# Gate and up projections of a decoder block: tokens as the stationary operand, weights as the moving one

## The chip, the cores and the metric

One core of a Trainium2 chip runs the whole block in one launch. The metric is the device time of one execution in microseconds (us). The three timed runs of the kernel before lie between 1873.48 and 1873.96 us, with the median at 1873.7 us.

## The reference

One decoder layer on 512 tokens with a model width of 2048, in float32. The first half (RMSNorm, three token mixers, output projection, residual) is not touched by the change. The second half is:

```python
h2 = _rms_norm(x, norm2_g[l])
x = x + (jax.nn.silu(h2 @ w_gate[l]) * (h2 @ w_up[l])) @ w_down[l]
```

`w_gate` and `w_up` are 2048 x 5632 (44 blocks of 128 hidden channels each), and `w_down` is 5632 x 2048.

## The kernel before, in words

The float32 products are made of three products of rounded parts (`F32R`): high x high, high x low, low x high. An operand tile `h` or `a` (128 x 512) therefore holds 256 columns of high parts and then 256 of low parts. Weights come from DRAM as plain float32 tiles of 128 x 1024 ("raw": `w('21', 'g10')` and so on). ScalarE rounds each of them twice (`wn` into PSUM, L293, and `wh` into SBUF, L294), and VectorE makes the low part `wl` (L295). The kernel calls one such tile in its split form a unit.

The three big products are done by a Strassen-Winograd scheme. Tokens are cut into two halves of 256, and the other two dimensions into two halves as well. Instead of eight block products there are seven, in the fixed order `ORDER = (5, 1, 7, 6, 2, 4, 3)`. The sums of weight blocks that the scheme needs (`s = 21+22`, `21 += 11`, `s += 11`, `s += 12`) are made by GpSimd (L200 for gate and up, L241 for down). The sums of the operands are made once, during the output projection that precedes (`operand`, L1100 to L1110), for all eight pairs of input blocks: 56 tiles `h`, of which `h7_3` is product 7, pair 3. They stay in SBUF through gate and up.

Gate and up (class `Wide`, L1308). There are 44 groups: pairs `p` of hidden blocks in `GU_ORDER`, gate first (`g10`) and then up (`u10`). A group has seven products, each with one unit. A product is 8 matmuls of 512 columns (`wh` stands in the array, the high and low columns of `h` move) and 8 of 256 columns (`wl` stands, the high columns move), all at L1292. Results lie with hidden channels on partitions. VectorE adds them out of PSUM (L1300 to L1334), GpSimd multiplies by the tokens' norm (`R_21`, L1258 and L1345), ScalarE applies SiLU, GpSimd multiplies gate and up. The pieces `sums1` to `piece4` then make the seven operand tiles `a` of the down projection. For all pairs but 0 and 5 (`STAY`) these tiles go out to DRAM (`od`) and are read back later.

Down. For the first 16 of 22 pairs (class `Turned`, 8 steps) it is done the other way round: blocks of 128 tokens of `a` stand, and 512 columns of weights move (L1434: 4 hidden or output blocks of 128 columns each). A step has 7 products with two units each, and a unit is 12 matmuls of 512 columns. Two banks are written per product, and the next product writes the other two. Its `a` tiles are read back from `od` every second step. The last 6 pairs (class `Down`) have the form of `Wide` again.

Order of the work: everything is written in program order per engine. `split_up_to` keeps the split `SPLIT_AHEAD = 2` units ahead of TensorE. `pump` issues weight loads on SP's queue as soon as a raw buffer of the right kind is free in the program's order. `later(n, ...)` puts work n products later, into `evacs` (emptying PSUM) or `extras` (the rest). All loads and stores stand in SP's one queue in program order, and SP waits in order. `SUMS_AT` says how many units ahead of a group each weight sum is made.

Of the kernel before, what the change touches and what calls it, by code (L numbers as in the profile page):

```python
# [53 lines left out]

SUMS_AT = {1: [(-4, -3, 0, 2)], 2: [(-5, -2, 1, 5), (-3, -1, 2, 6)]}
# [20 lines left out]
GU_ORDER = [*range(1, 5), *range(6, NP), 0, 5]  # L76
STAY = (0, 5)
# [6 lines left out]
RINGS = {"22": ("22a", "x0", "22b"), "s": ("sa", "x1", "sb"), "21": ("21", "x2"), "1": ("11", "x3", "12")}  # L84
# [38 lines left out]
def kernel(ctx: ExitStack, tc: tile.TileContext, xT, wi, wo, wgu, wd, cst_in, outT):  # L123
# [41 lines left out]
    first_sum, opening = [], f"g{GU_ORDER[0]}"  # L165
# [19 lines left out]

    def group(name, m, n, blocks):

        key = {k: (k, name) for k in ("11", "12", "21", "22", "s")}
        for k in ("21", "22", "11", "12"):
            entries.append((k + "ab"[m] if k == "22" else k, key[k], blocks[k]))  # L190
        u = len(works)

        def add(to, a, b, last=None):
            def go():
                if to == a:
                    out = raws[key[to]][0]
                else:
                    out = take("s" + "ab"[m], key[to], n)
                eng = nc.vector if name == opening and b == "11" and to == a == "s" else nc.gpsimd
                eng.tensor_add(out[:, :n], raws[key[a]][0][:, :n], raws[key[b]][0][:, :n])  # L200
                if last:
                    drop(key[last])
            return go

        sums[u - 4].append(add("s", "21", "22"))
        sums[u - 3].append(add("21", "21", "11"))
        if name == opening:
            first_sum.append((add("s", "s", "11"), key["11"]))
        else:
            sums[u].append(add("s", "s", "11", "11"))  # L210
        sums[u + 2 + (name == opening)].append(add("s", "s", "12"))
        works.extend((key[k], last, None) for k, last in (
            ("s", False), ("11", False), ("21", True), ("s", False), ("12", True), ("22", True), ("s", True)))

    for p in GU_ORDER:
        for m in range(2):
            group(f"{'gu'[m]}{p}", m, 1024, {f"{i + 1}{k + 1}": [wgu[4 * (p + i * NP) + 2 * m + k]]
                                             for i in range(2) for k in range(2)})
# [7 lines left out]
    def down_group(name, n, subs):  # L226
# [19 lines left out]
        for i in range(many):  # L246
            at_sum = SUMS_AT[many][i] if name != "d0" or i else (-4, *SUMS_AT[many][i][1:])
# [847 lines left out]
    x2d = {n: tc.dram_tile([P, T], F32, name=f"x2d{n}") for n in range(KT)}  # L1095

# [3 lines left out]
    def operand(q, j, src):  # L1100
        if q == 5 and j < N_WIDE:
            if j % 2 == 0:
                opening_ops[j] = wide(j + 1, f"h5_{j}", F32R)
            t = ops[q, j] = opening_ops[j - j % 2][:, j % 2 * T:(j % 2 + 1) * T]
        else:
            t = ops[q, j] = slot(f"h{q}_{j}", F32R)
        hi, lo = halves(t)
        nc.scalar.copy(hi, src)
        nc.vector.tensor_sub(lo, src, hi.bitcast(F32))

# [85 lines left out]
    for half in range(2):  # L1196
        for i, n in enumerate(OUT_ORDER[half]):
# [11 lines left out]
            if half == 1 and i == KT - 1:  # L1209
                drop(first_sum[0][1])  # L1210
            for kk in range(8):
                if half == 1 and i == KT - 2 and kk == 4:
                    first_sum[0][0]()
# [21 lines left out]
    r2b = cp.tile([P, 3 * TH], F32, name="r2b")  # L1235
    R_12, R_21, R_1, R_2 = r2b[:, :T], r2b[:, TH:], r2b[:, :TH], r2b[:, TH:T]
# [4 lines left out]
    def norm2a():  # L1241
        n2["b"] = psum["high"].tile([P, 1024], F32, name="n2s", tag="h")
        n2["r"] = token_scale(ssum2, D, "n2", n2["b"][:, :NT])[1]

    def norm2b():
        b = spread(n2["r"], "r2s", n2.pop("b")[:, T:])
        nc.scalar.copy(R_12, b)
        nc.scalar.copy(r2b[:, T:], b[:, :TH])
# [59 lines left out]
    class Wide(Block):  # L1308


        def __init__(self, p, m, gate):
            super().__init__(f"{'gu'[m]}{p}", m)
            self.p, self.gate = p, gate

        def done(self, q):
            if q == 1:
                self.u = slot(f"{self.name}u")
                self.u1, self.u2 = halves(self.u)
                self.both(1, self.u1)
            elif q == 7:  # L1320
                self.l, self.r = slot(f"{self.name}l"), slot(f"{self.name}r")
                self.both(7, self.r[:, :TH])
                self.add(5, self.r[:, :TH], sign=nc.vector.tensor_sub)
            elif q == 6:
                self.add(6, self.u2, self.u1)
                nc.gpsimd.tensor_sub(self.r[:, :TH], self.r[:, :TH], self.u2)
            elif q == 2:
                self.both(2, self.r[:, TH:])
                self.finish(self.r, self.gate and self.gate.r)
            elif q == 4:  # L1330
                c21 = self.l[:, TH:]
                main, rest = halves(self.banks[4])
                nc.vector.tensor_sub(c21, main, self.u2)
                nc.vector.tensor_add(c21, c21, rest)  # L1334
            elif q == 3:
                self.add(3, self.l[:, :TH], self.u2)
                self.u = self.u1 = self.u2 = None
                self.finish(self.l, self.gate and self.gate.l)
                if self.gate:
                    for n, piece in ((0, self.sums1), (1, self.piece3), (3, self.piece1), (4, self.sums2),  # L1340
                                     (6, self.piece2), (8, self.piece4)):
                        later(n, piece, queue=extras)

        def finish(self, t, gate):
            nc.gpsimd.tensor_mul(t, t, gate if gate is not None else R_21)  # L1345
            if gate is None:
                later(0, nc.scalar.activation, t, t, AF.Silu, queue=extras)
                later(1, nc.gpsimd.tensor_mul, t, t, R_21, queue=extras)


        def sums1(self):
            self.gate = None
# [11 lines left out]
        def piece(self, at, src):  # L1364
# [6 lines left out]
            for k in range(n):  # L1371
# [5 lines left out]
                if self.p in STAY:  # L1377
                    acts[q, self.p] = t
                else:
                    later(0, nc.sync.dma_start, od[self.p][:, (at + k) * T:(at + k + 1) * T], t.bitcast(F32),  # L1380
                          queue=extras)
# [121 lines left out]

    class Down(Block):
# [48 lines left out]
    def load_act(q, pairs):  # L1553
        for j in pairs:
            if j in STAY:
                continue
# [4 lines left out]
    blk = gate = None  # L1561
    rest = [(q, j) for q in ORDER for j in range(TURNED, NP)]
    for buf in ("x1", "x3"):
        held[buf] = "ops"
    for g in range(2 * NP + N_DOWN):
        t = g - 2 * NP
        turned = 0 <= t < N_TURNED
        if t < 0:
            p, m = GU_ORDER[g // 2], g % 2
            blk = Wide(p, m, gate if m else None)  # L1570
            gate = blk if m == 0 else None
        else:
            blk = (Turned if turned else Down)(t)
        for i, q in enumerate(ORDER):
            sums_now()
            run(evacs)
            for sub in range(BY // 2 if turned else 1):
                w = next_unit(SPLIT_AHEAD - (g == 0 and i == 2))
                if g == 0 and ticks.due:
                    for first in (0, NJ // 2):  # L1580
                        blk.multiply(q, w, [ops[q, j] for j in range(first, first + NJ // 2)], first, first > 0)
                        ticks.tick()
                elif t < 0:
                    blk.multiply(q, w, [ops[q, j] for j in range(NJ)])
# [5 lines left out]
            if g == 0 and i in (2, 3):  # L1590
                (norm2a, norm2b)[i - 2]()

            if t == -2 and i in (3, 6):
                load_act(ORDER[i // 6], range(BY))
            if t == -1:
                for j in range(NJ):
                    ops.pop((q, j))
                if i == 1:
                    held.pop("x1"), held.pop("x3")
                    opening_ops.clear()  # L1600
                if i < len(ORDER) - 2:
                    later(1 if i < len(ORDER) - 3 else 3, load_act, ORDER[i + 2], range(BY), queue=extras)
# [100 lines left out]
```

## Time and profile before

| | |
|---|---|
| median of 3 runs | 1873.7 us (1873.48 to 1873.96) |
| the profiled execution: its own time | 1876.25 us |
| the profiled execution: span of the core | 1874.5 us |
| TensorE busy in the span | 1867.3 us |
| VectorE, ScalarE, GpSimd busy | 1454.2, 1329.0, 1217.9 us |
| granted TensorE clock | 1.00 in every slice |
| moved by DMA | 301.07 MB, 161 GB/s on average |

The profile is one execution on the chip. Busy time is the union of an engine's instructions. Matmuls overlap: one of 512 columns is listed with 389 ns, and the next one starts 227 ns later, so a price of a matmul is read from starts or from counts per stretch and not from its duration. "PEld" is the loading of the standing operand, which overlaps with matmuls.

### The profile page before, as it was taken

The page shows a single profiled execution, that of the slowest core. Times are in us where ns is not written, and L with a number is a line of the kernel's source. Part 1 is how long each engine was busy: PE and PEld are TensorE (multiplying, and loading weights), DVE is VectorE, ACT ScalarE, POOL GpSimd, SP SyncE. Part 2 cuts the span into 40 slices and gives each one's busy share as a digit, 9 for nine tenths or more (in the row PEclk, how much of TensorE's full clock was granted, in tenths as well). Part 3 has the DMA queues.
Part 4 walks back from the last instruction along what each step waited for, and adds up shares of the span by engine and source line. Part 5 has one row for each costly group of instructions (what it writes and reads, how often), then busy time and mean ns, then how long its engine had stood idle before and what let it go on. Part 6 is the DMA issues. An engine that isn't in the chain of part 4 may idle for free.

```text
span 1874.5 us, 28274 instructions
## 1 busy us (share of the span) xinstructions
PE 1867.3 (100%) x9784; PEld 1604.5 (86%) x9784; DVE 1454.2 (78%) x2267; ACT 1329.0 (71%) x1870; POOL 1217.9 (65%) x796
## 2 busy tenths in 40 slices
PE   9999999999999999999999999999999999999999
PEld 7888888888888888888888888888888888888888
DVE  7688899897589777777777777777777677778887
ACT  6325556454466888888888888888888887777675
POOL 5003444362155887887878878778787767766786
PEclk9999999999999999999999999999999999999999
DMA  7334333433342353544535445354455465578984
GB/s 260 124 107 114 101 97 107 113 119 119 104 155 91 123 181 130 167 159 145 176 130 169 157 148 174 129 172 155 150 171 201 150 233 189 194 257 283 309 241 124
DMA packets 157984, 301.07 MB, mean 161 GB/s; under 512 B 29968, under 2 KB 69008, under 8 KB 157840
## 3 DMA queue, kind: packets, MB, share of 16 engines
q1 hardware_dynamic: 157696, 299.25, 48.8%
q8 instruction: 77, 1.26, 0.3%
q14 instruction: 67, 0.55, 0.1%
q10 hardware_dynamic: 144, 0.01, 0.0%
HBM read 241.27 MB, written 50.33 MB: 156 GB/s over the span
## 4 chain that ended last, share of the span: by engine, by line
PE 95%; DVE 3%; issue 1%; ACT 0%; DMA 0%; SPq 0%; DVEq 0%; ACTq 0%
PE out L1292 51%; PE out L1434 16%; PE o L332 2%; PE o L331 2%; PE o L333 2%; PE cq L331 2%; PE cq L332 2%; PE cq L333 2%; PE in L331 1%; PE in L332 1%; PE in L333 1%; PE aq L331 1%; PE bu L332 1%; PE aq L333 1%; PE bu L331 1%; PE bu L333 1%
## 5 line engine op out<-in xcount | busy, mean ns | idle before, releaser
L1292 PE MATMUL out<-h,wh 128*128 128x512 f32 x2464 | 588.4, 391 | 0.0
L1292 PEld LDWEIGHTS out<-h,wh 128*128 128x128 f32 x2464 | 452.7, 188 | 87.5
L1292 PEld LDWEIGHTS out<-h,wl 128*128 128x128 f32 x2464 | 316.2, 191 | 12.5 <-DVE wl L295 0.4
L1292 PE MATMUL out<-h,wl 128*128 128x256 f32 x2464 | 320.3, 283 | 0.2 <-DVE wl L295 0.2
L1434 PE MATMUL out<-wh,a 128*128 128x512 f32 x896 | 221.3, 389 | 0.0
L1434 PEld LDWEIGHTS out<-wh,a 128*128 128x128 f32 x896 | 168.2, 188 | 34.9
L1434 PE MATMUL out<-wl,a 128*128 128x512 f32 x448 | 119.7, 389 | 0.0
L1434 PEld LDWEIGHTS out<-wl,a 128*128 128x128 f32 x448 | 84.1, 188 | 17.4
L533 DVE SCALAR_TENSOR_TENSOR y<-bu,cst,y 128x511 f32<-128x511 f32 (+14 forms) x120 | 93.8, 782 | 1.4
L289 ACT CAST wh<-w 128x1024 fp32r<-128x1024 f32 (+1 forms) x41 | 42.1, 1032 | 59.0 <-PE o L332 34.5
L1292 PE MATMUL out<-a,wh 128*128 128x512 f32 x330 | 80.1, 391 | 0.0
L309 ACT CAST wh<-w 128x1024 fp32r<-128x1024 f32 x52 | 54.8, 1053 | 32.1 <-PE bg L332 9.0
L313 DVE TENSOR_TENSOR wl<-w,wh 128x1024 fp32r<-128x1024 f32 x52 | 65.3, 1257 | 14.2 <-ACT wh L309 13.9
L1292 PEld LDWEIGHTS out<-a,wh 128*128 128x128 f32 x330 | 60.2, 188 | 11.4
L290 DVE TENSOR_TENSOR wl<-w,wh 128x1024 fp32r<-128x1024 f32 (+1 forms) x41 | 51.6, 1260 | 11.9 <-ACT wh L289 11.7
L331 PE MATMUL o<-mh_c,wh 128*128 128x512 f32 x128 | 51.2, 400 | 0.0
L332 PE MATMUL o<-ml_c,wh 128*128 128x512 f32 x128 | 50.2, 392 | 0.1
L333 PE MATMUL o<-mh_c,wl 128*128 128x512 f32 x128 | 50.1, 392 | 0.0
L1479 DVE TENSOR_TENSOR Y<-Y,out 128x512 f32<-128x512 f32 x48 | 30.8, 683 | 19.4 <-PE out L1434 19.3
L1292 PEld LDWEIGHTS out<-a,wl 128*128 128x128 f32 x330 | 43.3, 191 | 2.2
L1292 PE MATMUL out<-a,wl 128*128 128x256 f32 x330 | 44.0, 283 | 0.0
L449 POOL TENSOR_TENSOR ssum<-ssum,sq 128x512 f32<-128x512 f32 x15 | 25.9, 1725 | 22.1 <-ACT sq L448 21.6
(3358 smaller groups left out, 5235.7 us busy)
## 6 DMA issues: line engine op xcount, KB each, us to landing
od<-a SPq DMA_DIRECT2D x140, 256.0 KB, 4.8
a<-od SPq DMA_DIRECT2D x140, 256.0 KB, 6.2
w<-in_wi SPq DMA_DIRECT2D x59, 512.0 KB, 3.5
w<-in_wo SPq DMA_DIRECT2D x32, 512.0 KB, 3.5
x<-in_xT SPq DMA_DIRECT2D x16, 256.0 KB, 7.1
xr<-in_xT SPq DMA_DIRECT2D x16, 256.0 KB, 3.9
x2d<-xr SPq DMA_DIRECT2D x16, 256.0 KB, 2.0
yd<-z SPq DMA_DIRECT2D x16, 256.0 KB, 5.3
```

The lines of the kernel that those rows point to most:

```text
L289: nc.scalar.copy(hi[:, :n], t[:, :n])
L290: eng.tensor_sub(lo[:, :n], t[:, :n], hi[:, :n].bitcast(F32))
L309: nc.scalar.copy(hi, t)
L313: nc.vector.tensor_sub(lo, t, hi.bitcast(F32))
L331: nc.tensor.matmul(out, wh, xh, start=start, stop=False)
L332: nc.tensor.matmul(out, wh, xl, start=False, stop=False)
L333: nc.tensor.matmul(out, wl, xh, start=False, stop=stop)
L449: eng.tensor_add(acc, acc, sq)
L533: nc.vector.scalar_tensor_tensor(yconv[j][:, i:], hconv[j][:, :T - i], c, yconv[j][:, i:], op0=ALU.mult, op1=ALU.add)
L1292: nc.tensor.matmul(out, lhs[:, s], rhs, start=begin, stop=last and low == flip[0] and x is xs[-1], skip_group_check=True)
L1434: nc.tensor.matmul(to[h], x[:, h * P:(h + 1) * P], v[:, j], start=sub == 0 and h not in started, stop=sub == 1 and n in (len(todo) - 1, le ...
L1479: nc.vector.tensor_add(t, t, b)
```

## The change

Gate and up take the form that the first 16 pairs of down have. The standing operand is now a block of 128 tokens of `h`, and 512 columns of weights move: 2 pairs x (gate, up) x 128 channels. `Wide` becomes a subclass of `Turned`, and there are 22 steps instead of 44 groups. Each step covers two pairs, but only half of the contraction: four of the eight pairs of input blocks, set 0 or set 1. Two steps in a row (even, then odd) complete two pairs. A step has 7 products of two units. The even step starts sums in SBUF (`G`), the odd one adds to them.

The result has tokens on partitions. SwiGLU is then done on token rows with the norm as a scalar per partition (ScalarE's SiLU with a scale, then one VectorE instruction). VectorE transposes 32 x 32 blocks (`z`), and the rest of the turn goes through DRAM: `z` is written to `zd`, and class `Pair` reads it back in runs of 64 floats (`f6r`, `f6l`). From there the pieces go on as before. All pairs now go through `od`; `STAY` is gone.

The operands `h` are also written to DRAM (`hd`) when they are made, since only one set stays in SBUF. From step 2 on, every even step reads the other set back, 28 tiles, one step ahead of its use. The set that a step uses goes 0, 1, 1, 0, 0, 1, 1, ...

```diff
-GU_ORDER = [*range(1, 5), *range(6, NP), 0, 5]
-STAY = (0, 5)
+G_STEPS = NP
+J_SET = NJ // 2
...
-RINGS = {"22": ("22a", "x0", "22b"), "s": ("sa", "x1", "sb"), "21": ("21", "x2"), "1": ("11", "x3", "12")}
+RINGS = {"22": ("22a", "x0", "22b"), "s": ("sa", "sb", "x1"), "21": ("21", "x2"), "1": ("11", "12", "x3")}
...
+    def set_of(g):
+        return (g + 1) // 2 % 2
+
+    def wide_block(g, i, k, j):
+        return [bass.AP(tensor=wgu.tensor, offset=wgu.offset + (4 * (2 * (g // 2) + i * NP) + k) * P * 1024 + j * P,
+                        ap=[[1024, P], [2 * P * 1024, 4], [1, 2 * P]])]
+
+    for g in range(G_STEPS):
+        down_group(f"w{g}", 8 * P, [{f"{i + 1}{k + 1}": wide_block(g, i, k, J_SET * set_of(g) + 2 * sub)
+                                     for i in range(2) for k in range(2)} for sub in range(2)])
...
         nc.vector.tensor_sub(lo, src, hi.bitcast(F32))
+        ticks.after(1, nc.sync.dma_start, hd[j][:, LAID.index(q) * T:(LAID.index(q) + 1) * T], t.bitcast(F32))
...
+    class Pair:
+        def load(self, side, d):
+            t = slot(f"{self.name}{side}")
+            nc.sync.dma_start(t.rearrange("p (k a x) -> p k a x", k=2, a=4),
+                              bass.AP(tensor=d.tensor, offset=d.offset + self.p % 2 * P * 64,
+                                      ap=[[64, P], [P * T, 2], [32 * T, 4], [1, 64]]))
...
+    class Wide(Turned):
+        def done(self, q, banks):
+            y, u, name = self.y, self.u, f"G{self.g}"
+            if self.first:
+                if q in (5, 1, 7):
+                    new = y[{5: "12", 1: "11", 7: "21"}[q]] = self.pair(f"{name}_{q}")
+                    for t, b in zip(new, banks):
+                        nc.scalar.copy(t, b)
...
+            else:
+                for to, op in {5: (("12", nc.vector.tensor_add), ("22", nc.vector.tensor_sub)),
+                               1: (("u", nc.vector.tensor_add), ("11", nc.vector.tensor_add)),
+                               7: (("21", nc.vector.tensor_add), ("22", nc.vector.tensor_add)),
+                               6: (("u", nc.vector.tensor_add),)}.get(q, ()):
+                    for t, b in zip(u if to == "u" else y[to], banks):
+                        op(t, t, b)
+            if q in (2, 4, 3):
+                for t, b in zip(y[{2: "11", 4: "21", 3: "12"}[q]], banks):
+                    nc.vector.tensor_add(t, t, b)
...
+            for part in {6: ("22",), 2: ("11",), 4: ("21",), 3: ("12",)}.get(q, ()):
+                later(1, self.finish, part, queue=extras)
...
+        def finish(self, at):
...
+                nc.scalar.activation(out, both[:, :, 0], AF.Silu, scale=scale)
+                nc.vector.scalar_tensor_tensor(out, both[:, :, 1], scale, out, op0=ALU.mult, op1=ALU.mult)
+                nc.vector.transpose(to[:, :, h], one.rearrange("p (c b) -> p b c", b=8))
...
+                if t == -1:
+                    later(1, load_act, q, range(BY), queue=extras)
+                elif g:
+                    later(1, load_ops, q, 1 - set_of(g), queue=extras)
```

TensorE, the middle of gate and up, before: the end of the high half and the low half of one product of `g10` (`h` moves, a 128 x 128 block of `wh` or `wl` stands).

```order
L1292 MATMUL out_5765<-h_6_5731,wh_9095 128x512
L1292 MATMUL out_5765<-h_7_5815,wh_9095 128x512
L1292 MATMUL out_5765<-h_0_5041,wl_9096 128x256
L1292 MATMUL out_5765<-h_1_5204,wl_9096 128x256
L1292 MATMUL out_5765<-h_2_5307,wl_9096 128x256
L1292 MATMUL out_5765<-h_3_5409,wl_9096 128x256
L1292 MATMUL out_5765<-h_4_5510,wl_9096 128x256
```

TensorE after: the end of the first unit of one product of step 8 and the start of its second (`wh` and `wl` move, a block of 128 tokens of `h` stands).

```order
L1379 MATMUL out_5827<-wh_8902,h_1_8267 128x512
L1379 MATMUL out_5828<-wh_8902,h_1_8267 128x512
L1379 MATMUL out_5827<-wl_8903,h_0_8265 128x512
L1379 MATMUL out_5827<-wl_8903,h_1_8267 128x512
L1379 MATMUL out_5828<-wl_8903,h_0_8265 128x512
L1379 MATMUL out_5828<-wl_8903,h_1_8267 128x512
L1379 MATMUL out_5827<-wh_8921,h_2_8269 128x512
```

The 256-column form is gone, and two banks are written in turn. Two groups were 224 matmuls; a step is 168, all with 512 columns.

VectorE before, in the middle of group `g10` (`u9tb`, `u9n` and `a_9` are pieces of the pair 9 before it):

```order
L295 TENSOR_TENSOR wl_9228<-w('s', 'g10')_8988,wn_9229 128x1024
L1300 TENSOR_REDUCE g10r<-out_5764 128x256
L295 TENSOR_TENSOR wl_9256<-w('s', 'u10')_9186,wn_9257 128x1024
L1333 TENSOR_TENSOR g10l<-out_5765,g10u 128x256
L1334 TENSOR_TENSOR g10l<-g10l,out_5765 128x256
L295 TENSOR_TENSOR wl_9281<-w('11', 'u10')_9105,wn_9282 128x1024
L1375 TENSOR_TENSOR a_9_9304<-u9tb,u9n_9302 128x4x2x32
```

VectorE after, in the first two products of the odd step 9 (`G` are the sums, `f6` and `f7` the pairs 6 and 7 on their way to `a`):

```order
L1479 TENSOR_TENSOR G_50_8953<-G_50_8953,out_5827 128x512
L1479 TENSOR_TENSOR G_51_8954<-G_51_8954,out_5828 128x512
L1479 TENSOR_TENSOR G_220_9073<-G_220_9073,out_5827 128x512
L1479 TENSOR_TENSOR G_221_9074<-G_221_9074,out_5828 128x512
L273 TENSOR_TENSOR wl_9370<-w('21', 'w9', 0)_8963,wn_9371 128x1024
L273 TENSOR_TENSOR wl_9392<-w('21', 'w9', 1)_8985,wn_9393 128x1024
L1323 TENSOR_TENSOR a_6_9413<-f6l,f6n_9411 128x4x2x32
L1323 TENSOR_TENSOR a_7_9418<-f7r,f7n_9416 128x4x2x32
L1323 TENSOR_TENSOR a_7_9421<-f7r,f7n_9416 128x4x2x32
```

Emptying PSUM now stands in blocks of four 512-wide additions ahead of the `wl` of the next product.

SP's queue before, around the loads of `g10`:

```order
L277 DMA w('21', 'g10')_8907<-in_wgu 128x1024
L277 DMA w('22', 'g10')_8909<-in_wgu 128x1024
L277 DMA w('11', 'g10')_8911<-in_wgu 128x1024
L1258 DMA od_5775<-a_8_8890 128x512
L1258 DMA od_5775<-a_8_8893 128x512
L277 DMA w('12', 'g10')_8969<-in_wgu 128x1024
L1258 DMA od_5775<-a_8_8956 128x512
L277 DMA w('21', 'u10')_9101<-in_wgu 128x1024
```

SP's queue after, in the first two products of the even step 8:

```order
L1237 DMA zd_1_8510<-z_11_8891 128x512
L1295 DMA f6r<-zd_1_8510 128x8x64
L255 DMA w('21', 'w9', 0)_8963<-in_wgu 128x4x256
L255 DMA w('22', 'w9', 0)_8965<-in_wgu 128x4x256
L255 DMA w('21', 'w9', 1)_8985<-in_wgu 128x4x256
L1295 DMA f7r<-zd_1_8510 128x8x64
L1575 DMA h_4_9009<-hd_3893 128x512
L1575 DMA h_5_9011<-hd_3894 128x512
L1575 DMA h_6_9013<-hd_3895 128x512
L1575 DMA h_7_9015<-hd_3896 128x512
L1237 DMA zd_0_8509<-z_21_8942 128x512
```

Reads of `zd` (which must wait for the writes just ahead of them) and of `hd` now stand between the weight loads, and weights come in runs of 256 floats instead of 1024.

More of the change, by code (lines that the diff above doesn't have):

```diff
@@ L184 @@
         works.append((u, True, nc.vector))
[L186 to L218, printed above, removed]
     turn = defaultdict(int)
@@ L1095 @@
     x2d = {n: tc.dram_tile([P, T], F32, name=f"x2d{n}") for n in range(KT)}
+    hd = {j: tc.dram_tile([P, 7 * T], F32, name=f"hd{j}") for j in range(NJ)}
+    for buf in ("x1", "x3"):
+        held[buf] = "ops"
     def halves(t):
@@ L1306, in add @@
             sign(out, out, rest)
[L1308 to L1348, printed above, removed]
@@ L1351, in sums1, with __init__ @@
+    class Pair:
+        def __init__(self, p):
+            self.name, self.p = f"f{p}", p
+        def load(self, side, d):
[3 more added lines that the diff above has]
+                                      ap=[[64, P], [P * T, 2], [32 * T, 4], [1, 64]]))
+            setattr(self, side, t)
         def sums1(self):
[L1352 removed]
@@ L1376, in piece @@
                                      tokens(near[:, s].bitcast(F32), "a b c"))
[L1377 to L1381, printed above, removed]
+                later(0, nc.sync.dma_start, od[self.p][:, (at + k) * T:(at + k + 1) * T], t.bitcast(F32),
+                      queue=extras)
         def piece1(self):
@@ L1576 @@
             run(evacs)
[L1577 to L1581, printed above, removed]
+            for sub in range(BY // 2 if t < N_TURNED else 1):
+                w = next_unit()
+                if t < 0:
+                    first = J_SET * set_of(g) + 2 * sub
+                    blk.multiply(i, sub, w, [ops[q, j] for j in range(first, first + 2)])
+                    if ticks.due:
                         ticks.tick()
-                elif t < 0:
-                    blk.multiply(q, w, [ops[q, j] for j in range(NJ)])
                 elif turned:
```

99 lines of the change are left out of this document (64 added, 35 removed).

## The prediction, made before the changed kernel was run

> **What bounds the kernel now.** I read the busy times and the chain first, then stretches of the two stages that matter: gate and up (700 to 1300 us), and the part of down that already has the new form (1500 to 1700 us).
>
> ```profile
> PE 1867.3 (100%) x9784; PEld 1604.5 (86%) x9784; DVE 1454.2 (78%) x2267; ACT 1329.0 (71%) x1870; POOL 1217.9 (65%) x796
> ...
> PE 95%; DVE 3%; issue 1%; ACT 0%; DMA 0%; SPq 0%; DVEq 0%; ACTq 0%
> ```
> ```profile
> core 0: us, PE busy (x) PEld busy (x) DVE busy (x) ACT busy (x) POOL busy (x), PEclk, DMA share, GB/s
> 700.00:1300.00 600.00, 600.00 (x3452) 530.30 (x3451) 451.21 (x662) 495.05 (x630) 480.81 (x309) 1.00 0.46 155
> 1500.00:1700.00 200.00, 200.00 (x884) 165.68 (x883) 145.71 (x168) 152.91 (x164) 137.64 (x72) 1.00 0.67 228
> 1580.00:1600.00 20.00, 20.00 (x90) 16.58 (x89) 14.88 (x18) 15.50 (x16) 16.52 (x10) 1.00 0.96 340
> ...
> 1740.00:1760.00 20.00, 20.00 (x98) 16.86 (x97) 14.90 (x20) 13.15 (x17) 16.23 (x12) 1.00 1.04 351
> 1760.00:1800.00 40.00, 40.00 (x232) 35.33 (x231) 38.46 (x70) 29.89 (x38) 32.99 (x26) 1.00 0.90 256
> ```
>
> TensorE never pauses in either stage and its clock is full, so only fewer or cheaper matmuls, or a new stall, can move the end. The counts give prices. In gate and up a matmul starts every 600/3452 = 173.8 ns (half are 512 wide, half 256). In the turned stage, all 512 wide, one starts every 200/884 = 226.2 ns.
>
> **The change, part by part.** (1) *Matmuls.* The stage and one product in it:
>
> ```profile
> L1292 PE MATMUL out<-h,wh x2464: 388/389/477, 590.3 to 1449.1; 128*128 128x512 f32 x190
> L1292 PE MATMUL out<-h,wl x2464: 277/283/387, 591.2 to 1447.4; 128*128 128x256 f32 x190
> ```
> ```profile
> 901.97 3.82 PE L1292 MATMUL out<-h,wh 128*128 128x512 f32 x16
> ...
> 905.40 2.09 PEld L1292 LDWEIGHTS out<-h,wl 128*128 128x128 f32 x16
> 905.62 2.08 PE L1292 MATMUL out<-h,wl 128*128 128x256 f32 x16
> ...
> 907.54 3.82 PE L1292 MATMUL out<-h,wh 128*128 128x512 f32 x16
> ```
>
> Sixteen wide ones take 905.62 - 901.97 = 3.65 us (228 ns each), sixteen narrow ones 1.92 us (120 ns). Half of a wide one would be 114 ns or less, and the weight loads of the narrow ones fill their time (2.09 of 1.92 us, overlapping): a narrow matmul pays for a standing block that only 256 columns use. Before: 4928 x 173.8 ns = 856.5 us. After: 22 steps x 168 = 3696 matmuls x 226.2 ns = 836.0 us, since the turned stage has the same instruction with the same shapes. Gain 20.5 us; a step is 38.0 us, a product 5.43 us. [...]
>
> (2) *VectorE and ScalarE*, per two steps (76.0 us), against two old pairs (four groups, 448 matmuls, 77.9 us).
>
> ```profile
> L295 DVE TENSOR_TENSOR wl<-w('s', 'g10')_8988,wn 128x1024 fp32r<-128x1024 f32 x3 | 3.6, 1216 | 0.8 <-PE out L1292 0.8
> L1479 DVE TENSOR_TENSOR Y<-Y,out x48: 649/682/702, 1476.3 to 1754.3; 128x512 f32<-128x512 f32 x48
> L1498 DVE STREAM_TRANSPOSE z<-Y x32: 622/654/701, 1709.2 to 1787.4; 128x256 f32<-128x256 f32 x32
> 904.01 0.42 DVE L1305 TENSOR_TENSOR u9l<-u9u,out 128x256 f32<-128x256 f32 x1 [0.79 <-PE out L1292]
> 909.58 0.69 DVE L1300 TENSOR_REDUCE g10u<-out 128x256 f32<-128x512 f32 x1 [0.85 <-PE out L1292]
> L533 DVE SCALAR_TENSOR_TENSOR y<-bu,cst,y 128x511 f32<-128x511 f32 (+14 forms) x120 | 93.8, 782 | 1.4
> L1451 ACT COPY Y<-out x4: 589/592/594, 1454.5 to 1493.6; 128x512 f32<-128x512 f32 x4
> L1258 ACT ACTIVATE g1r<-g1r x1: 633/633/633, 611.4 to 611.4; 128x512 f32<-128x512 f32 x1
> L1374 ACT CAST a<-u1r x2: 402/404/405, 634.7 to 635.0; 128x256 fp32r<-128x256 f32 x2
> L1375 DVE TENSOR_TENSOR a<-u1r,u1n x2: 414/414/415, 635.2 to 635.6; 128x256 fp32r<-128x256 f32 x2
> ```
>
> VectorE was busy 451.21/600 = 75.2%, or 58.6 us of the 77.9. The old emptying goes: four groups x (3 x 0.69 + 8 x 0.42) = 21.7 us. New: 10 additions of 512 in the even step and 20 in the odd, 30 x 0.682 = 20.5 us; 8 SwiGLU instructions of 256, bounded by 0.42 and 0.78 us (I take 0.45, since half of 511 columns is nearer to the first); 8 transposes x 0.654. Sum 58.6 - 21.7 + 20.5 + 3.6 + 5.2 = 66.2 us, 87% (91% at the upper bound). ScalarE: 495.05/600 = 82.5%, 64.3 us; plus 6 copies x 0.592, plus 8 SiLUs of 256 at about 0.40 (as the 256-wide cast) for 4 x 0.633: 68.5 us, 90%. GpSimd loses the multiplications by the norm and gains six 512-wide sums, and falls. Nothing is over TensorE on average, so I charge 0.
>
> The average hides a hump. In the seven products whose emptying belongs to the odd step, VectorE has 20 x 0.682 + 14 x 1.216 + 8 pieces x 0.414 + three finishes x 2 x 1.10 = 40.6 us against 38.0. Overlap between neighbours makes it less. The excess of at most 2.6 us has cover: the split runs two units (one product, 5.4 us) ahead, and the two pairs of banks alternate. If that cover is gone, 11 odd steps cost up to 29 us.
>
> (3) *DMA.* Per two steps: weights 16 x 0.524 MB, `h` 28 x 0.262, `od` 14 x 0.262, `zd` 4 written and 4 read: 21.5 MB in 76 us, 283 GB/s.
>
> ```profile
> q1 hardware_dynamic: 32987, 92.30, 45.9%
> ```
> ```profile
> GB/s 361 331 151 343 376 25 262 288 28 3 288 132 0 96 84 310 385 237 355 384 254 229 277 125 0 209 215 0 19 93 313 386 248 334 376 332 152 383 358 364
> ...
> q1 hardware_dynamic: 35025, 45.36, 66.3%
> ...
> a<-od SPq DMA_DIRECT2D x88, 256.0 KB, 6.3
> ...
> w('12', 'd2', 0)_15493<-in_wd SPq DMA_DIRECT2D x1, 512.0 KB, 8.8
> ```
>
> The first row is gate and up's 600 us, the second fence the turned stage's 200 us in 5 us slices. The turned stage has the same weight runs and the same 28 reads per two steps. Its price is 0.663 x 200 / 45.36 = 2.92 us per MB. The window 1760 to 1800 us, where `yd` is read in the short runs that `zd` will have, gives 0.90 x 40 / (0.256 x 40) = 3.5. So the 21.5 MB take 63 to 75 us of 76. They are uneven. The stretch of seven products in which `h` is read also has 8 weight tiles and 11 other transfers: 14.4 MB, 42 us at 2.92 (50 at 3.5) against 38. The other stretch has 7.1 MB. So a backlog of some 4 us builds up and drains. [...]
>
> What waits for the backlog? `h` is read six products (33 us) ahead. Weights are nearer: the second `22` of a step is issued about half-way through the step before and its sum is due some two products later.
>
> ```profile
> ACT wh L294 <- PE out L1434: 35.0, 49, 0.8
> ...
> POOL w('s', 'd3', 0)_15837 L241 <- DVE wl L295: 8.1, 1, 8.1
> ```
> ```profile
> POOL w('s', 'g7')_7746 L200 <- DMA w('22', 'g7')_7667<-in_wgu: 3.2, 1, 3.2
> ```
>
> In the turned stage GpSimd's sums wait up to 8.1 us for VectorE to be done with a buffer; the list of its waits has no row in which they wait for a load, though loads land up to 8.8 us after issue at 0.96 of the DMA. In gate and up a load was late by 3.2 us once, and TensorE did not notice. So lateness of 4 us is hidden: charge 0, bounds 0 and 4 to 12 us for each of the ten reading steps. SP also waits in order, before `f6r` and `f6l`, for the `zd` writes just ahead; weights stand behind them:
>
> ```profile
> yd<-z SPq DMA_DIRECT2D x16, 256.0 KB, 5.3
> ```
>
> By this neighbour that is some 5 us of SP twice per two steps, again less than one product.
>
> (4) *Opening and end.* 56 `hd` writes join SP's queue in the output projection, where the DMA is little used, but VectorE is full:
>
> ```profile
> 580.00:590.00 10.00, 10.00 (x46) 8.29 (x45) 10.00 (x15) 5.19 (x10) 2.77 (x3) 1.00 0.14 52
> 590.00:600.00 10.00, 10.00 (x63) 8.94 (x63) 9.60 (x21) 8.19 (x16) 0.00 (x0) 1.00 0.27 96
> 600.00:610.00 10.00, 9.82 (x56) 8.36 (x55) 8.10 (x13) 6.58 (x9) 8.90 (x5) 1.00 0.39 142
> ```
>
> The first step needs only the operands of set 0, so the late ones (pair 7) get a step of grace; one 1024-wide sum leaves VectorE. Against that, `w0`'s last tiles stand in SP's queue behind `hd` writes that wait for VectorE. Bounds: -0.2 us (the pause there) and +10 us (two products). I take 0, nearer to the row. At the end of gate and up the last reading step meets the first loads of `a`, 28 tiles more; same cover.
>
> *Sum.* The profiled execution took 1876.25 us (span 1874.5); less 20.5 gives 1855.8 and a span of 1854. The median of the runs is 2.55 us lower: 1853.2, said as 1853.5.
>
> **The rivals.**
>
> *A. DMA lateness reaches TensorE (slower).* Place: the seven products in which `h` is read, through the weight sums on GpSimd and `wn` on ScalarE. For it: 14.4 MB against 38 us, short runs, and SP's in-order waits. Against: the turned stage at 0.96. It decides from about 2 us lost per reading step (10 x 2 = 20.5). At 4.1 us: 1853.5 + 41 = 1894; at 12, 1973.
>
> *B. VectorE and ScalarE stall each other in the odd steps.* Each `wn` needs a PSUM buffer that VectorE must release, and each SwiGLU waits for ScalarE's SiLU. For it: 40.6 us against 38.0 and ScalarE at 90%. Against: VectorE is at 38.46 of 40 us in 1760 to 1800, and TensorE is whole there. Price 1 to 2.6 us x 11: 1865 to 1882, across the line.
>
> *C. The opening costs up to 10 us:* 1863, still faster.
>
> *D. The matmul price does not change.* If the 120 ns are not a surcharge of narrowness but follow the stage, columns alone count. They are equal: 4928 / 2 x 768 = 3696 x 512. [...]
>
> **How the numbers follow.** No stall 0.64, C 0.06, A 0.16, B 0.10, D 0.04. A difference under 0.2% (3.7 us) can't be told from no change. Faster: no stall, C, and the third of B below 1870: 0.73. Same: D, a third of B, and a little of A: 0.09. Slower: most of A and the last third of B: 0.18. The range: down to 1848 (the wide one at 225 ns and 2.4 us of the opening gained), up to 1884, which takes in C, D, B and A's mild end, and leaves out A's rest.
>
> **What would show it.** Right: 442 matmuls per 100 us all through gate and up, a stage of some 836 us, VectorE near 87%, ScalarE near 90%, DMA near 283 GB/s at 0.83 to 0.99, no idle TensorE. Wrong: idle TensorE behind `wl` or `wh`, recurring every 76 us; with GpSimd's sums waiting for loads of `22` or `11` it is A, with VectorE saturated in the odd steps it is B, only before the first product it is C. Steps of 38.9 us without pauses would be D.

## The result: 1950.2 us, 4.1% slower

The changed kernel takes 1950.21 us (median of 5 runs, 1949.1 to 1954.71) against 1873.7 us; the ratio is 1.0411, with an interval from 1.0396 to 1.0426. The forecast of 1853.5 us missed by 97 us, and the range (to 1884) did not hold it.

The page of the changed kernel, with its busy times and the chain of waits, then the window from 700 to 1300 us that was read in the kernel before, and a window without disturbance (columns as in the prediction):

```profile
PE 1879.6 (97%) x8548; PEld 1544.1 (79%) x8548; DVE 1580.7 (81%) x2290; ACT 1372.3 (70%) x1978; POOL 1103.1 (57%) x687
...
PE 26%; DMA 3%; DVE 2%; ACT 2%; SPq 1%; issue 1%; POOL 0%; DVEq 0%; ACTq 0%; POOLq 0%
```
```profile
700.00:1300.00 600.00, 564.33 (x2401) 452.55 (x2400) 492.62 (x627) 488.52 (x657) 364.03 (x211) 0.99 0.78 256
620.00:660.00 40.00, 40.00 (x178) 33.14 (x177) 30.70 (x37) 29.14 (x30) 18.67 (x10) 1.00 0.35 106
```

Where nothing disturbs, the price is the forecast one: 178 matmuls in 40 us are 225 ns each. But in 700 to 1300 us TensorE lacks 36 us, and only 400 matmuls per 100 us start, not 442. In the chain, DMA, ScalarE and SP's queue have come in (its listed shares stop at 35% of the span). What TensorE waits for:

```profile
PE out L1379 <- DVE G L1482: 26.2, 20, 2.3
PE out L1379 <- ACT wh L272: 23.0, 10, 3.5
PE out L1379 <- ACT wh L267: 5.4, 1, 5.4
PE out L1379 <- ACT Y L1397: 3.7, 1, 3.7
```

From the starts of the stage's 3696 matmuls one can work out what each product takes over 24 x 226.5 ns = 5.44 us. Steps count from 0; in the expectations, "the pauses of the even steps" are the loss that the table has at the start of an odd step, and "the end of every odd step" is part of its first column. Three places carry nearly all of the loss, and the experiments below are read by the same table (us; the first two columns are means per two steps, over steps 4 to 19):

| kernel | around the start of an even step | start of an odd step | whole first step | stage | time |
|---|---|---|---|---|---|
| changed | 3.75 | 4.47 | 9.3 | 927.1 | 1950.2 |
| e1 SiLU in PSUM | 1.58 | 2.61 | 9.3 | 888.0 | 1908.2 |
| e2 reads of `zd` later | 5.60 | 0.0 | 9.4 | 902.9 | 1924.7 |
| e3 no read-back of `h` | 1.31 | 0.0 | 9.3 | 862.7 | 1883.8 |
| e12 e1 and e2 | 3.16 | 0.0 | 9.3 | 875.3 | 1895.5 |
| e1s e1, both SiLUs first | 0.44 | 4.90 | 9.4 | 897.2 | 1915.4 |
| m1 e1s and e2, second pair's pieces back | 0.0 | 0.0 | 9.3 | 847.1 | 1863.1 |
| m5 m1, opening changed | 0.0 | 0.0 | 3.5 | 841.4 | 1857.4 |

An undisturbed stage is 837 us. The stage lost 90 us; the turned stage behind it lost another 6 at its start (310.4 us against m1's 304.5).

**Around the start of an even step.** Timelines of VectorE, GpSimd and TensorE there:

```profile
836.81 2.25 DVE L1511 SCALAR_TENSOR_TENSOR s<-G,n2r,s 128x256 f32<-128x256 f32 x1 [0.33 <-ACT s L1510]
839.09 0.68 DVE L1512 STREAM_TRANSPOSE z<-s 128x256 f32<-128x256 f32 x1
839.70 1.90 DVE L1511 SCALAR_TENSOR_TENSOR s<-G,n2r,s 128x256 f32<-128x256 f32 x1
...
842.20 1.25 DVE L1482 TENSOR_TENSOR G<-G,out 128x512 f32<-128x512 f32 x2
...
836.38 2.38 POOL L207 TENSOR_TENSOR w('s', 'w6', 0)_7971<-w('21', 'w6', 0)_7787,w('22', 'w6', 0)_7789 128x1024 f32<-128x1024 f32 x1
838.74 2.58 POOL L207 TENSOR_TENSOR w('s', 'w6', 1)_8021<-w('21', 'w6', 1)_7809,w('22', 'w6', 1)_7951 128x1024 f32<-128x1024 f32 x1
...
843.00 2.39 PE L1379 MATMUL out<-wh,h 128*128 128x512 f32 x8 [1.15 <-DVE G L1482]
```

The SwiGLU instruction (L1511), forecast at 0.45 us, takes 2.25 and 1.90 us, and each time it ends 0.3 us behind the GpSimd sum that it met (836.38 + 2.38 = 838.76 against 836.81 + 2.25 = 839.06). The emptying of the bank, L1482, stands behind it on VectorE, and TensorE waits for that. Its neighbour L1512, which reads one operand, is not slowed (0.68 us). Of the 88 instructions L1511, the 44 that overlap with a GpSimd sum average 1.77 us, the other 44 0.46 us.

**Start of an odd step**, behind a read-back. SP's queue, and then who waits for whom:

```profile
868.99 0.32 SPq L1237 DMA_DIRECT2D zd<-z  x1
874.26 0.37 SPq L1295 DMA_DIRECT2D f4l<-zd  x1
874.68 3.30 SPq L1575 DMA_DIRECT2D h<-hd  x4
878.09 0.38 SPq L255 DMA_DIRECT2D w('22', 'w7', 1)_8339<-in_wgu  x1
...
885.44 2.36 POOL L207 TENSOR_TENSOR w('s', 'w7', 1)_8417<-w('21', 'w7', 1)_8191,w('22', 'w7', 1)_8339 128x1024 f32<-128x1024 f32 x1 [17.30 <-DMA w('22', 'w7', 1)_8339<-in_wgu]
...
887.84 1.02 ACT L271 CAST wn<-w('s', 'w7', 1)_8417 128x1024 fp32r<-128x1024 f32 x1 [9.43 <-POOL w('s', 'w7', 1)_8417 L207]
...
889.88 3.06 PE L1379 MATMUL out<-wh,h 128*128 128x512 f32 x8 [3.50 <-ACT wh L272]
```

SP stands still for 5 us, until the write of `zd` has landed that `f4l` reads; four reads of `h` go next, and the weight tile `22` behind them is issued at 878.09 and lands about 885.4, 7.3 us later. GpSimd waits, then ScalarE, then TensorE: rival A, at the place that the prediction named.

**The opening.** VectorE, GpSimd and TensorE before the second product:

```profile
585.16 2.62 DVE L1091 TENSOR_TENSOR h<-ta,h 128x256 fp32r<-128x256 f32 x1
587.70 0.67 DVE L1106 TENSOR_TENSOR xr<-xr,o 128x512 f32<-128x512 f32 x1
588.30 2.83 DVE L268 TENSOR_TENSOR wl<-w('s', 'w0', 1)_5701,wh 128x1024 fp32r<-128x1024 f32 x1
...
591.39 2.61 DVE L1091 TENSOR_TENSOR h<-ta,h 128x256 fp32r<-128x256 f32 x1
...
584.92 2.58 POOL L207 TENSOR_TENSOR w('21', 'w0', 1)_5377<-w('21', 'w0', 1)_5377,w('11', 'w0', 1)_5538 128x1024 f32<-128x1024 f32 x1
587.46 2.59 POOL L207 TENSOR_TENSOR w('s', 'w0', 0)_5592<-w('s', 'w0', 0)_5592,w('11', 'w0', 0)_5430 128x1024 f32<-128x1024 f32 x1
591.21 2.51 POOL L207 TENSOR_TENSOR w('s', 'w0', 1)_5701<-w('s', 'w0', 1)_5701,w('11', 'w0', 1)_5538 128x1024 f32<-128x1024 f32 x1 [1.16 <-DVE wl L268]
...
599.95 3.78 PE L1379 MATMUL out<-wh,h 128*128 128x512 f32 x8 [5.42 <-ACT wh L267]
```

The same sign: an operand's low part (L1091, 0.41 us alone) takes 2.6 us beside a sum of the new first weights, and ends 0.28 us behind it.

### The profile page after: what moved, and what is told of

Its sections match the earlier page's. It is cut to its first block, busy times and chain, and to the rows that moved or that the text cites. A ratio compares the mean times of both kernels' runs of the same rounds, so it can differ in the third digit from the quotient of the medians.

```text
span 1947.3 us, 26832 instructions
## 1 busy us (share of the span) xinstructions
PE 1879.6 (97%) x8548; PEld 1544.1 (79%) x8548; DVE 1580.7 (81%) x2290; ACT 1372.3 (70%) x1978; POOL 1103.1 (57%) x687
## 5 line engine op out<-in xcount | busy, mean ns | idle before, releaser
L1379 PE MATMUL out<-wh,h 128*128 128x512 f32 x2464 | 630.7, 397 | 56.3 <-DVE G L1482 26.2
L1379 PEld LDWEIGHTS out<-wh,h 128*128 128x128 f32 x2464 | 464.4, 190 | 177.6 <-ACT wh L272 32.3
L1379 PE MATMUL out<-wl,h 128*128 128x512 f32 x1232 | 331.9, 391 | 0.0
L1379 PEld LDWEIGHTS out<-wl,h 128*128 128x128 f32 x1232 | 233.8, 190 | 49.5
L1511 DVE SCALAR_TENSOR_TENSOR s<-G,n2r,s 128x256 f32<-128x256 f32 x88 | 98.2, 1116 | 4.3 <-ACT s L1510 4.3
L1482 DVE TENSOR_TENSOR G<-G,out 128x512 f32<-128x512 f32 x132 | 83.7, 675 | 16.9 <-PE out L1379 16.9
L287 ACT CAST wh<-w 128x1024 fp32r<-128x1024 f32 x52 | 54.7, 1053 | 32.1 <-PE bg L310 9.0
L1479 DVE TENSOR_TENSOR G<-G,out 128x512 f32<-128x512 f32 x110 | 68.5, 680 | 1.7 <-PE out L1379 1.7
L1512 DVE STREAM_TRANSPOSE z<-s 128x256 f32<-128x256 f32 x88 | 59.0, 670 | 3.0
```

The lines of the kernel that those rows point to most:

```text
L287: nc.scalar.copy(hi, t)
L1379: nc.tensor.matmul(to[h], x[:, h * P:(h + 1) * P], v[:, j], start=sub == 0 and h not in started, stop=sub == 1 and n in (len(todo) - 1, le ...
L1479: op(t, t, b)
L1482: nc.vector.tensor_add(t, t, b)
L1511: nc.vector.scalar_tensor_tensor(out, both[:, :, 1], scale, out, op0=ALU.mult, op1=ALU.mult)
L1512: nc.vector.transpose(to[:, :, h], one.rearrange("p (c b) -> p b c", b=8))
```

## The experiments

**e1: SiLU in PSUM.** One operand of the SwiGLU instruction moves to PSUM.

```diff
+silu = psum["high"].tile([P, 1024], F32, ...)
-nc.scalar.activation(out, both[:, :, 0], AF.Silu, scale=scale)
-nc.vector.scalar_tensor_tensor(out, both[:, :, 1], scale, out, ...)
+nc.scalar.activation(gate, both[:, :, 0], AF.Silu, scale=scale)      # gate lies in silu
+nc.vector.scalar_tensor_tensor(out, both[:, :, 1], scale, gate, ...)
```

> ScalarE writes the SiLU into a PSUM tile instead of SBUF, so that the SwiGLU instruction has one operand in PSUM and one in SBUF; nothing else changes. Theory T1 (the SwiGLU instruction with both operands in SBUF is held up while GpSimd runs a sum; it takes 1.77 us beside GpSimd and 0.46 us without): every one of the 88 takes about 0.46 us, the two pauses of TensorE of 1.5 and 1.8 us at the end of every odd step go with the half-rate matmuls behind them (3.75 us per two steps), and the time falls by some 35 to 40 us, to 1910 to 1916 us. Rival R1 (VectorE is simply overfull in the odd steps, and the long instructions are a symptom): the instruction may shorten but VectorE still has the same work to wait behind; at most 10 us, 1940 to 1950. The pause in the even steps stays under both.

Measured: 1908.2 us, ratio 1.0183 (1.0168 to 1.0199), 42.0 us less than the changed kernel. The group of the instruction in the changed kernel and in e1:

```profile
L1511 DVE SCALAR_TENSOR_TENSOR s<-G,n2r,s 128x256 f32<-128x256 f32 x88 | 98.2, 1116 | 4.3 <-ACT s L1510 4.3
```
```profile
L1513 DVE SCALAR_TENSOR_TENSOR s<-G,n2r,g 128x256 f32<-128x256 f32 x88 | 40.7, 463 | 6.6 <-ACT g L1512 3.7
```

Sixty-five of e1's 88 still lie beside a GpSimd sum, and take 0.464 us there. So it is not GpSimd's presence that costs, but two operands in SBUF at that time (1.77 us). T1 holds. It gained a little more than expected, since the odd steps' start fell too (4.47 to 2.61 us).

**e2: reads of `zd` one product later**, with the sums and pieces behind them.

```diff
-later(k, one.load, "r", ...)        later(3 + k, one.load, "l", ...)        later(n + 4 * k, piece, ...)
+later(1 + k, one.load, "r", ...)    later(4 + k, one.load, "l", ...)        later(n + 1 + 4 * k, piece, ...)
```

> The reads of zd (f6r, f6l and their kind), and the sums and pieces that use them, are put one product later in the program; no byte more or less is moved. Theory T2a (SP stands up to 5 us in front of such a read until the write of zd just ahead has landed, and the raw weights behind it come too late for GpSimd's sum): SP's wait falls from about 4 us to under 1 us each, the pauses of the even steps (4.3 us per two steps) go, and the time falls by 30 to 43 us, to 1907 to 1920 us. Theory T2b (there are too many bytes in the stretch in which h is read back, the waits of SP are only where the lateness shows): SP's wait goes elsewhere, and the time stays within 10 us, 1940 to 1950 us.

Measured: 1924.7 us, ratio 1.0270 (1.0255 to 1.0286), 25.5 us less: between the two. SP's waits for the write of `zd`, in the changed kernel and in e2:

```profile
SPq L1295 <- DMA zd<-z: 102.4, 27, 4.9
```
```profile
SPq L1295 <- DMA zd<-z: 3.8, 4, 2.9
```

The loss at the odd steps' start is gone to the last tenth (T2a), but the even steps' start became dearer (3.75 to 5.60 us). That the moved pieces did this is argued here; m1, which puts half of them back, has no such loss, but its SwiGLU is another as well.

**e3: no read-back of `h`.**

```diff
-first = J_SET * set_of(g) + 2 * sub
+first = J_SET * (g > 0) + 2 * sub
...
-elif g:
-    later(1, load_ops, q, 1 - set_of(g), queue=extras)
```

> h is not read back: from the second step on every step uses the four pairs of set 1, which stay in SBUF (so the products leave out set 0 there and are not the reference's); weights, instructions of the engines and reads of zd are as in the changed kernel. Both T2a and T2b expect the pauses of the even steps gone, since the late weights stand behind reads of h: 43 us less, 1900 to 1915 us. If SP's wait before the reads of zd is enough by itself to make the weights late (T2a in its strict form), half or more of the even-step pauses stay, and it is 1925 to 1950. The pauses at the end of the odd steps stay under all.

Measured: 1883.8 us, ratio 1.0059 (1.0042 to 1.0076), 66 us less, better than either theory said. SP's wait and the DMA in e3:

```profile
SPq L1295 <- DMA zd<-z: 102.0, 22, 5.7
```
```profile
700.00:1300.00 600.00, 594.64 (x2609) 488.73 (x2608) 528.77 (x683) 535.35 (x713) 406.21 (x237) 1.00 0.60 184
```

SP waits as long as in the changed kernel (102 us), yet no weight is late enough to be felt. So the wait alone does not do it, and by e2 the bytes alone do not either: lateness needs both, 5 us of SP standing still and then reads of `h` ahead of the weight tile. The second lesson: the even steps' start fell from 3.75 to 1.31 us, though L1511 still takes 1.00 us on average:

```profile
L1511 DVE SCALAR_TENSOR_TENSOR s<-G,n2r,s 128x256 f32<-128x256 f32 x88 | 88.3, 1003 | 0.8 <-ACT s L1510 0.8
```

Two thirds of that loss went with the read-back. That GpSimd's sums, once late, bunch where VectorE has its SwiGLU is my reading; no run tests it by itself, and in e2, where the weights were in time as well, the loss grew.

**e12: both mended.**

> The SiLU in PSUM and the later reads of zd together. If T1 and T2a hold and the two losses are independent, the gains add: some 39 + 40 us, 1868 to 1880 us, with only the pauses of the opening (8 us) and the start of the turned stage (4 us) left. If T2b holds, 1900 to 1915.

Measured: 1895.5 us, ratio 1.0117 (1.0102 to 1.0132): above the 1868 to 1880 of independent gains, 54.7 less where 67.5 would be the sum of e1 and e2. What is left stands at the even steps' start, with ScalarE in front: a second SiLU waits there 0.55 us for the first SwiGLU instruction, as both halves lie in one PSUM tile (ScalarE's timeline of e12), and the moved pieces are in the way:

```profile
986.50 0.48 ACT L1512 ACTIVATE g<-G,n2r 128x256 f32<-128x256 f32 x1 [0.55 <-DVE s L1513]
```

**m1 and e1s: the order on ScalarE.** e1s issues both SiLUs before the first SwiGLU instruction; m1 also has the later reads, with the second pair's pieces at their old places (`n + (4 if k else 1)`).

> As e12 (SiLU in PSUM, reads of zd one product later), with two changes of order: ScalarE makes both halves' SiLU before the first SwiGLU instruction is issued (in e12 the second SiLU waits 0.55 us for the first SwiGLU, since both lie in one PSUM tile), and the pieces of the second pair go back to their old places. What is left in e12 is 2.85 us at the start of every even step, in its first three products, with ScalarE busy there all the time. Theory T4 (ScalarE is overfull there by its waits and by the pieces that were moved in): 25 to 30 us go, 1866 to 1871 us. Rival R4 (ScalarE's own work there, six weight tiles at 2.1 us, copies and SiLU, is too much for three products in any order): at most 10 us go, 1885 to 1895.

> m1 without the later reads of zd: the SiLU in PSUM, both before the SwiGLU instruction, reads and pieces where the changed kernel has them. With SwiGLU and ScalarE's waits mended, is SP's wait before the reads of zd still a loss? If lateness of the weights reaches TensorE by itself (T2a or T2b), the pause at the start of the steps behind a read-back (2.6 us of loss per two steps in e1) stays: 1880 to 1890. If it only did so because GpSimd and ScalarE were late for other reasons, the time is within 3 us of m1's: 1860 to 1866.

Measured: m1 1863.1 us, ratio 0.9941 (0.9928 to 0.9953): T4 holds (which of its two changes did how much isn't separated), and no step but the first loses anything. e1s 1915.4 us, ratio 1.0223 (1.0209 to 1.0237): not in either expectation. By m1 - e1s, lateness of the weights is worth 52 us when all else is mended, more than the 43 us seen at first. Why e1s is 7 us behind e1 is open; in the table it gains 1.1 us at the even steps' start and loses 2.3 at the odd ones'. m1's page and window:

```profile
PE 94%; DVE 3%; ACT 1%; issue 1%; DMA 0%; DVEq 0%; ACTq 0%
```
```profile
700.00:1300.00 600.00, 600.00 (x2649) 496.99 (x2648) 508.35 (x697) 544.46 (x727) 404.51 (x238) 1.00 0.86 282
```

This is the picture that the prediction drew: 441.5 matmuls per 100 us, VectorE 85%, ScalarE 91%, DMA 282 GB/s at 0.86, no idle TensorE.

**o1 and m2: the opening, first try.** ScalarE also rounds the operands (and `w0`'s first four units) into PSUM, for VectorE to subtract from.

```diff
+near = by_block(psum["high"].tile([P, 1024], F32R, ...)[:, :TH])
+nc.scalar.copy(near, src)
 nc.scalar.copy(hi, src)
-nc.vector.tensor_sub(lo, src, hi.bitcast(F32))
+nc.vector.tensor_sub(lo, src, near.bitcast(F32))
```

> Only the opening is changed, against the changed kernel: from the third tile of the output projection's second half on, ScalarE also rounds each operand into a PSUM tile, and VectorE subtracts that one, so that the making of a low part has one operand in SBUF instead of two; the first four weight tiles of gate and up are split in the same way. Theory T3 (the low parts of the operands, 0.42 us alone and up to 2.62 us beside a GpSimd sum of w0, hold VectorE up before the first products): these instructions take about 0.42 us, the pause of 5.8 us behind the first product and the half-rate matmuls after it go, and the time falls by 7 to 10 us, to 1940 to 1943. Rival R3 (VectorE or ScalarE is full there without any holding up): under 3 us gained, or something lost by ScalarE's 0.4 us more for each operand, 1947 to 1953.

> m1 and o1 together. With T1 to T4 true, steps of 38.05 us throughout and no pause in the opening: 1857 to 1862 us, faster than the kernel before (1873.9) by 0.6 to 0.9%, which is what the price of the matmuls alone promised. If the opening's gain is lost again behind ScalarE, 1866 to 1871.

Measured: o1 1950.9 us, ratio 1.0410 (1.0396 to 1.0424), no gain, inside R3's range; m2 1865.9, ratio 0.9953 (0.9939 to 0.9967), 2.8 us behind m1. The first step lost more than before, 13.6 us in o1 and 13.4 in m2. The low parts did become 0.42 us each, but the next instructions with two SBUF operands took their place beside the same sums, as o1's VectorE shows:

```profile
585.72 2.62 DVE L1141 TENSOR_TENSOR ta<-h,h 128x256 f32<-128x256 f32 x1
588.44 2.44 DVE L1142 TENSOR_TENSOR tb<-ta,h 128x256 f32<-128x256 f32 x1
590.91 0.42 DVE L1143 TENSOR_TENSOR tb<-tb,h 128x256 f32<-128x256 f32 x1
```

**m3 and m3c: take the sums away from there instead.** Three (m3) or four (m3c) of `w0`'s sums go to VectorE, behind the operands.

```diff
-FIRST_SUMS_AT = [(-4, -2, 1, 5), (-2, -1, 2, 6)]
+FIRST_SUMS_AT = [(-4, -2, 4, 5), (-2, 3, 5, 6)]
...
-nc.gpsimd.tensor_add(out[:, :n], ...)
+early = name == "w0" and b == "11" and (to == "s" or i == 1)
+(nc.vector if early else nc.gpsimd).tensor_add(out[:, :n], ...)
```

> m1, and three of the eight sums of the first step's weights (s += 11 twice, and 21 += 11 for the second unit) go from GpSimd to VectorE (1.22 us each), one to two products later in the program, so that no GpSimd sum runs while VectorE makes the last operands (two SBUF inputs). The run o1 took the low parts out of GpSimd's way and the pause only moved: VectorE's sums ta and tb (0.42 us alone) then took 2.62 and 2.44 us beside GpSimd. Theory T3b (it is this holding up of VectorE, whichever two-input instruction meets it, that delays ScalarE's casts and so the second product): the pause of 5.8 us goes, the first step loses 0 to 3 us instead of 9.3, and the time is 1854 to 1858 us. Rival R3b (56 stores, 28 more operands' worth of work and the norm fill VectorE and ScalarE there anyway): 1861 to 1864.

> As m3, with the fourth sum (21 += 11 for the first unit) moved to VectorE too, behind the operands. T3b expects a microsecond or two more, from the low parts that take 2.62 us beside it some 13 us before the first product: 1853 to 1857. R3b: 1861 to 1864.

Measured: 1862.9 and 1863.0 us, ratio 0.9942 (0.9928 to 0.9955) and 0.9941 (0.9928 to 0.9953): no gain over m1, inside R3b's range. But the pause behind the first product was gone; the first step lost 9.8 and 10.7 us further on, as m3's TensorE shows:

```profile
604.43 2.11 PE L1381 MATMUL out<-wh,h 128*128 128x512 f32 x8 [0.78 <-ACT wh L274]
611.80 1.86 PE L353 MATMUL n2s<-ones,ssum2b 128*128 128x1 f32 x8 [4.34 <-DVE ssum2b L1228]
```

The eight small matmuls of the norm stand in TensorE's order behind the third product, and their input stands behind the moved sums on VectorE.

**m5 and n1: the norm later**, with (m5) and without (n1) the moved sums.

```diff
-if g == 0 and i == 2:
-    norm2()
+if g == 0 and i in (4, 6):
+    (norm2a if i == 4 else norm2b)()     # VectorE's copies, then the small matmuls
```

> m3 with the norm of the tokens two to four products later: VectorE's copies of ssum2 behind the fifth product, the small matmuls and the scale behind the seventh. In m3 the pause of 5.8 us behind the first product was gone, but TensorE then waited up to 6.5 us, behind the third product, for ssum2b on VectorE, which had the moved sums ahead of it. The scale is first used in the second step. Theory T3b with this wait taken away: the first step loses at most 3 us in place of 9.3 and the time is 1854 to 1858 us. If the wait is only handed on to the next product once more, 1861 to 1864.

> m1 with the norm later, and the weight sums on GpSimd as in m1. T3b expects the pause of 5.8 us behind the first product to stay and only the one of 2 us behind the third to go: 1860 to 1862 us. If the norm alone is what the opening loses by (the rival to T3b), 1854 to 1858.

Measured: m5 1857.4 us, ratio 0.9908 (0.9893 to 0.9923); n1 1861.6 us, ratio 0.9930 (0.9918 to 0.9942), with the pause behind the first product in its old place. The two low parts that took 2.6 us in the changed kernel, in m5:

```profile
585.05 0.41 DVE L1093 TENSOR_TENSOR h<-ta,h 128x256 fp32r<-128x256 f32 x1
...
587.46 0.41 DVE L1093 TENSOR_TENSOR h<-ta,h 128x256 fp32r<-128x256 f32 x1
```

VectorE is through with the second at 587.87 us, in the changed kernel at 594.00. T3b holds for the pause behind the first product: it was VectorE held up by GpSimd's sums, with the norm as the next wait behind it. What makes the 3.5 us that m5's first step still loses is open. m5 is faster than the kernel before by 0.9%.

## Why the prediction was wrong, by its own steps

- **(1) Matmuls, gain 20.5 us: right.** m1's steps take 38.05 us where 38.0 was said. m5 gains 16.3 us against the kernel before, and the 3.5 us that its first step still loses make it 19.8. Rival D fell: its sign was steps of 38.9 us.
- **(2) SwiGLU, 0.45 us with bounds 0.42 and 0.78: mis-sized, and with it the charge of 0.** It measured 1.116 us on average. The 3.6 us for eight became 8.9 us per two steps, and they fall at the one place where TensorE waits for VectorE. Rival B foresaw the place, but took sums of durations for its price: 1 to 2.6 us per two steps, where 3.75 were lost. Its lower bound came from 256-wide instructions that read one operand from PSUM (`out`, `u1n`), and with one operand there, as e1 showed, the SwiGLU instruction is not held up (0.464 us beside a sum). The trace of before had the upper end, in the opening:

```profile
566.83 2.61 DVE L1109 TENSOR_TENSOR h<-tb,h 128x256 fp32r<-128x256 f32 x1
...
566.59 2.57 POOL L200 TENSOR_TENSOR w('s', 'g1')_5547<-w('21', 'g1')_5293,w('22', 'g1')_5348 128x1024 f32<-128x1024 f32 x1
```

  An instruction that is 0.42 us elsewhere ends there 0.28 us behind GpSimd's sum. And the kernel's own `wn` in PSUM, written beside `wh` at the price of a second rounding, gives the making of `wl` one operand in PSUM, the remedy of e1: before, `wl` (L295) takes 1.22 us at most beside a sum (L200). Beside a sum the SwiGLU instruction took 1.77 us with both operands in SBUF (changed kernel), and 0.464 us with one in PSUM (e1).
- **(3) DMA and SP's waits, charge 0: wrong.** The rates were right (282 GB/s at 0.86 once the stalls were gone). The step that failed is "less than one product": two delays were each held against one product's slack, the backlog of 4 us and SP's 5 us, and not added. SP's 5.3 us (868.99 to 874.26), 3.3 us of reads of `h` and 7.3 us to land make 16 us for a tile that GpSimd waited 17.3 us for. Rival A was priced at 4.1 us per reading step; it was 4.5 in the changed kernel and 5.2 by m1 against e1s. A's sign and place were right. The chances let only one rival come; A, C and the place of B came together.
- **(4) Opening, bounds -0.2 and +10, taken as 0: wrong end.** It cost 9.3 us. Of these, 5.8 went in m5, where the sums no longer hold VectorE up (the hindrance of (2)) and the norm comes later. The stores of `hd` in SP's queue, the reason given for the upper bound, stood unchanged meanwhile; whether they have a part in the 3.5 us that are left, no run shows.
- Around the misses the sum closes: 1950.2 - 1857.4 = 92.8 us, of which m1 gives back 87.1 and the opening 5.7.

## What to carry to other kernels

Price an instruction of VectorE by what runs on GpSimd beside it: look up the longest of its kind in the trace and not the mean, and count its operands in SBUF; one operand in PSUM made 1.77 us into 0.46 us here. Add the delays that stand in one queue ahead of a load (a wait in order, the transfers in front, its own landing) before comparing them with the slack. A stall that is mended can show its neighbour: here three separate ones hid a gain of 16 us (m5), and single repairs gained 0 to 42 us, in sums that did not add up.

## What the runs showed of the hardware

TensorE's pauses cost more than themselves here. In the stage, the 31 pauses over 0.1 us take 60 of the 90 us; the other 30 are lost between matmuls that follow each other without one, and of these some 12 us lie in spells at a granted clock of 0.50. The changed kernel behind idle times of 1.39 and 1.84 us, and then three pairs of neighbouring stretches of 3.41 us:

```profile
973.09 2.11 PE L1379 MATMUL out<-wh,h 128*128 128x512 f32 x8 [1.39 <-ACT wh L272]
...
804.56 3.08 PE L1379 MATMUL out<-wh,h 128*128 128x512 f32 x8 [1.84 <-ACT wh L272]
```
```profile
802.01:805.41 3.40, 1.56 (x8) 0.97 (x7) 1.60 (x3) 2.90 (x5) 3.40 (x4) 1.00 1.16 316
805.42:808.83 3.41, 3.41 (x10) 2.64 (x9) 3.04 (x6) 3.41 (x5) 3.41 (x3) 0.50 1.05 379
887.34:890.75 3.41, 0.87 (x4) 0.74 (x5) 1.62 (x3) 2.92 (x5) 3.41 (x4) 1.00 1.08 313
890.75:894.16 3.41, 3.41 (x10) 2.63 (x9) 3.04 (x6) 3.41 (x5) 3.41 (x3) 0.50 1.04 380
1225.26:1228.67 3.41, 1.94 (x8) 1.61 (x9) 2.69 (x5) 3.41 (x6) 3.41 (x4) 1.00 1.14 322
1228.67:1232.08 3.41, 3.39 (x15) 2.46 (x14) 2.83 (x3) 2.95 (x4) 3.33 (x3) 1.00 1.05 386
```

After the 1.39 us eight matmuls take 2.11 us in place of 1.98 (7 x 226.5 + 389 ns), and after the 1.84 us, where the clock falls within them, 3.08. The length of the pause alone does not decide here: one of 2.29 us that ends at 683.46 us leaves the clock at 1.00. The spells at 0.50 in the steps behind the first begin at 805.42, 890.75, 1058.00, 1143.34, 1310.59 and 1395.92 us, last 3.41 us each, and lie 25 or 49 times 3.413 us apart. Counted back from them in steps of 3.413 us, a border falls at 682.54 us, within the pause that ends at 683.46 us, and cuts it into 1.37 and 0.92 us. In the first stretch of each pair above TensorE is idle for 1.84, 2.54 and 1.47 us; the first two are followed by 0.50, the third is not. With the changed kernel's trace cut at these borders, from 50 to 1942 us, each of the nine stretches with 1.84 us idle or more is followed by 0.50, and none with 1.47 us or less is. What sets the lengths and the distances, no run shows.

GpSimd's sums are longer too, but little: in the changed kernel those of the weights (L207) take 2.51 us on average where an L1511 lies beside them, and 2.32 where neither it nor an instruction of the operands or their splitting does.
